# Order of exponential and scaling in a softmax that runs beside a projection

## Chip, cores and metric

The kernel runs on one core of a Trainium2 chip. The metric is the time of one execution on the device in microseconds, the median of several runs. The core has one engine for matrix products (TensorE, PE in the profile, whose weight loads are shown as PEld), three for elementwise work (VectorE or DVE, ScalarE or ACT, GpSimd or POOL) and SyncE (SP), which issues most loads here. Each engine works through its own instructions in the order in which the program gives them; semaphores tie the engines together.

## The reference

One layer of a transformer on 256 tokens of width 1024: eight heads of blockwise attention of width 64 and four heads of retention of width 128 side by side, gated and merged, then a feed-forward block with a short convolution, each followed by a layer norm. With 256 tokens and a block of 256 there is one block, so the attention is plain causal attention:

```
l_own = jnp.einsum('bhqd,bhkd->bhqk', qc, k_own).astype(jnp.float32) * scale
l_own = jnp.where(causal, l_own, NEG_BIG)
...
p = jax.nn.softmax(logits, axis=-1).astype(v.dtype)
p_own = p[..., :MOBA_BLOCK]
...
return (jnp.einsum('bhqk,bhkd->bhqd', p_own, v_own) + ...)
```

What the change touches is the softmax of these eight heads.

## The kernel before

The program is one list of about 60 and more **steps** of matrix products over streamed weights (`steps`), and beside it generators (`sides`) that add small work between them. A weight tile of 128 x 2048 (`raw`, four buffers) is loaded by SyncE, split into two halves, and each half into a high part `whi` (ScalarE, line 1264) and a rest `wlo` (VectorE, line 1278), so that products have more than the precision of one pass. A buffer of `raw` is loaded again as soon as VectorE has read its last half; some loads (`in_ada`) feed a product on VectorE alone (line 263). The loop at line 1320 prepares halves some five ahead of their use, and `whi` one more ahead.

Steps 0 to 15 are the projections to queries and keys (`wstat_rot`, TensorE lines 134 and 138). Each pair of steps uses two of the four banks 0 to 3 of the accumulator memory in turn, and ScalarE copies each result out (line 504). Two steps of this kind hold 16 matmuls of line 134 and 16 of line 138. From step 16 on come steps of 12 matmuls (lines 123 to 125): `winB`, `winGa`, `winGr`. Rotations of the projected heads run on VectorE (lines 1006 to 1012).

The attention is the generator `mixers` (line 1029). Each step calls it three times, and its loop variable `i` is the step less 7 (`SCORES_AT`). The first call does nothing. The second, ahead of the step's matmuls in program order, holds ScalarE's exponentials and scalings. The third, behind the matmuls, holds VectorE's reciprocals, TensorE's transposes and scores, and VectorE's maxima:

- `scores(h)` (line 1050) forms the scores of four heads in banks 4, 7, 5, 6.
- `maxima(h)` (line 1059) adds the mask and scale for two heads, writes the scores out of the banks into a buffer of six heads (`sms`), and takes the row maxima.
- The exponential (line 1086) of a head subtracts the maximum and sums the rows; the reciprocal (line 1090) inverts the sums; the scaling (line 1082) multiplies the head by it.
- The transposes (line 1098) turn a head's scaled probabilities through a bank, and line 1100 copies them out. `attend` (line 1072) multiplies them by the values, at `i = 12`, after step 19. `retention` (from line 1114) follows and uses banks 4, 7, 0, 1 and then 5, 6.

In the kernel before, at each `i` the head `i - 2` is scaled and then head `i - 1` gets its exponential. Heads 0 and 1 are transposed at `i = 5` (step 12), 2 to 5 at 8 (step 15), 6 and 7 at 10 (step 17). Maxima are taken at `i = 0, 2, 4, 5`.

Of the kernel before, what the change touches and what calls it, by code (L numbers as in the profile page):

```python
# [9 lines left out]
AF = mybir.ActivationFunctionType  # L10
# [3 lines left out]
HM, DM = 8, 64  # L14
# [54 lines left out]
def _body(nc, a, out, pe, act, dve, sp, cst, wts, big, tmp, ps, dram):  # L69
    f = lambda ap: ap.bitcast(F32)  # L70

    def bank(i):
        return ps.tile([128, 512], F32, tag=f"P{i}", name=f"P{i}")
# [10 lines left out]
    def slot(n, shape, dt=F32):  # L84
        if n in pairs:
            assert pairs[n].dtype == dt
            return pairs[n].rearrange("p e (k t) -> p e k t", k=shape[2])
        if n not in place:
            return big.tile(shape, dt, tag=f"A{n}", name=f"A{n}")
        pair, e = place[n]  # L90
        assert pairs[pair].dtype == dt
        v = pairs[pair][:, e, :math.prod(shape[1:])]
        return v.rearrange("p (a b) -> p a b", a=shape[1]) if len(shape) == 3 else v
# [5 lines left out]
    def split(hi, lo, src):  # L99
        act.activation(hi, src, AF.Copy)  # L100
        dve.tensor_tensor(lo, src, f(hi), OP.subtract)
# [927 lines left out]
    def mixers():  # L1029


        for _ in range(3 * SCORES_AT):
            yield
        v = S["v"]
        S["decay"] = [slot(n, [128, 2, 384]) for n in ("6a", "6b")]
        for i in range(2):
            nc.gpsimd.dma_start(S["decay"][i], a["decay"][i])
        st, pt = {}, {}
        blk = [slice(128 * qb, 128 + 256 * qb) for qb in range(2)]

        def scores(h):


            S["sc"] = [bank(b) for b in (4, 7, 5, 6)]
            x = S["rot"][h // 4]
            for qb, c in enumerate(blk):
                for i in range(2):
                    for e in range(4):
                        s = slice(32 * e, 32 * e + 32)
                        pe.matmul(S["sc"][e][:, c], x[s, i, qb * 128:(qb + 1) * 128], x[s, 2 + i, :128 + 128 * qb],  # L1050
                                  start=i == 0, stop=i == 1)

        def maxima(h):

            for e in range(2):
                sm = S["sms"][:, (h + e) % (TL + 2)]
                mx = tmp.tile([128, 8], F32, name="mx", bufs=TL + 2)
                for qb, c in enumerate(blk):
                    dve.tensor_tensor_reduce(out=sm[:, c], in0=S["sc"][h % 4 + e][:, c],  # L1059
                                             in1=consts["mask"][:, 128 - 128 * qb:],  # L1060
                                             scale=-0.125, scalar=3.0e38, op0=OP.add, op1=OP.min,
                                             accum_out=mx[:, 2 + qb:3 + qb])
                st[h + e] = sm, mx

        def attend(h, p):

            for w in range(2):
                pT = [pt.pop(h + 2 * w + e) for e in range(2)]
                for kb, (o, c) in enumerate(((slice(0, 256), slice(0, 256)), (slice(128, 256), slice(256, 384)))):
                    for e in range(2):  # L1070
                        u = h + 2 * w + e
                        pe.matmul(p[64 * e:64 * e + 64, 256 * w + o.start:256 * w + o.stop],  # L1072
                                  v[:, kb, 64 * u:64 * u + 64], pT[e][:, c], start=kb == 0, stop=kb == 1)
            return lambda: split(S["yah"][:, h // 2:h // 2 + 2], S["yal"][:, h // 2:h // 2 + 2],
                                 p.rearrange("p (w t) -> p w t", w=2))

        for i in range(HM + 5):
            yield
            if 0 <= i - 2 < HM:
                sm, mx = st[i - 2]  # L1080
                for qb, c in enumerate(blk):
                    act.activation(sm[:, c], sm[:, c], AF.Copy, scale=mx[:, 6 + qb:7 + qb])
            if 0 <= i - 1 < HM:
                sm, mx = st[i - 1]
                for qb, c in enumerate(blk):
                    act.activation(sm[:, c], sm[:, c], AF.Exp, scale=-1.0, bias=mx[:, 2 + qb:3 + qb],
                                   accum_out=mx[:, 4 + qb:5 + qb])
            yield
            if 0 <= i - 1 < HM:
                dve.reciprocal(mx[:, 6:8], mx[:, 4:6])  # L1090
            if i == HM + 4:
                S["yah"], S["yal"] = [slot(n, [128, 4, 256], F32R) for n in ("5", "15")]
                done = [attend(4 * g, bank(5 + g)) for g in range(2)]
            for h in {5: (0, 1), 8: (2, 3, 4, 5), 10: (6, 7)}.get(i, ()):
                sm, mx = st.pop(h)
                p = bank((4, 7, 4, 7, 5, 6, 5, 6)[h])
                for b in range(3):
                    pe.transpose(p[:, b * 128:(b + 1) * 128], sm[:, b * 128:(b + 1) * 128], ident)
                pT = sm if h > 1 else slot(("9a", "9b")[h], [128, 384])
                act.activation(pT, p[:, :384], AF.Copy)  # L1100
                pt[h] = pT
            if i == 0:
                S["sms"] = slot(11, [128, TL + 2, 384])
            if i in (0, 4):
                scores(i)
            if i in (0, 2, 4, 5):
                maxima(i + i % 2)
            if i == RET_AT:
                sides.append(retention())
            yield  # L1110
        for fn in done:
            fn()
# [192 lines left out]
    prep_to(FIRST + 2)  # L1305
    evac_B()
    sides = [mixers()]

    def run_sides():
# [148 lines left out]
```

## Time and profile before

| | |
|---|---|
| median of 3 runs | 427.67 us (426.02 to 428.06) |
| the profiled execution | 427.91 us |
| its span | 426.2 us |
| mean granted clock of TensorE | 0.996 |
| busy: VectorE, ScalarE, GpSimd | 87%, 59%, 3% of the span |
| bytes read from memory | 104.28 MB, 247 GB/s over the span |

The span runs from the first to the last instruction that the profiler records; what is left of the execution's time lies around it. An engine's busy share is an average over stages; the softmax lies at about 85 to 133 us, and what it costs is read from the waits there. In the rows of the prediction, times are microseconds from the start of the span, `x` counts merged instructions, and `<-` in brackets names what ended an idle time. A row of a merged group gives its first start and the time to its last end; matmuls overlap, so the time that one takes is read from differences of starts.

### The profile page before, as it was taken

To read this page: it belongs to the slowest core of one execution; us is meant where nothing else is said; L and a number is where in the kernel's file an instruction comes from. 1 tells how busy PE (TensorE), PEld (TensorE's weight loads), DVE (VectorE), ACT (ScalarE), POOL (GpSimd) and SP (SyncE) were. 2 spreads that over 40 slices of the span, in tenths; PEclk is the share of its full clock that TensorE was granted. 3 is DMA by queue.
4 is the path that set the end of the run, shared out by engine and by line. 5 is a ranking of instruction groups with operands and counts; after the bars stand their busy time and mean duration, and the time that the engine had idled before them with its cause. 6 is when DMAs were issued, how large, how long until landed. Compare 5 with 4: busy or idle time off the path is not lost.

```text
span 426.2 us, 5934 instructions
## 1 busy us (share of the span) xinstructions
PE 414.9 (97%) x2156; PEld 348.4 (82%) x2156; DVE 370.6 (87%) x593; ACT 252.1 (59%) x442; POOL 14.0 (3%) x26
## 2 busy tenths in 40 slices
PE   7999999997989999999999999999999999999995
PEld 4888888886867888888888888888888888888884
DVE  5979788888988779799788889999999998689996
ACT  4666558658977498635433895374545555456700
POOL 0000010000000100000000000100000000003200
PEclk9999999999989999999999999999999999999999
DMA  8998999675486687979873064796757778550002
GB/s 290 408 408 334 408 397 413 247 245 195 155 297 228 257 304 285 334 269 345 297 256 140 0 235 161 274 363 252 291 211 287 295 250 289 205 197 2 0 2 99
DMA packets 18685, 105.73 MB, mean 248 GB/s; under 512 B 2272, under 2 KB 3680, under 8 KB 7904
## 3 DMA queue, kind: packets, MB, share of 16 engines
q1 hardware_dynamic: 17136, 99.84, 62.5%
q0 software_dynamic: 1376, 4.99, 3.4%
q10 hardware_dynamic: 144, 0.52, 0.5%
q8 instruction: 17, 0.28, 0.2%
q14 instruction: 12, 0.10, 0.1%
HBM read 104.28 MB, written 1.06 MB: 247 GB/s over the span
## 4 chain that ended last, share of the span: by engine, by line
PE 88%; DVE 8%; ACT 2%; DMA 1%; issue 0%; DVEq 0%; ACTq 0%
PE P L134 21%; PE P L337 13%; PE P L123 12%; PE P L125 12%; PE P L124 12%; PE P L138 11%; DVE wlo L1278 2%; DVE junk L263 2%; DMA raw<-in_m 1%; DVE A L1059 1%; PE P L721 1%; PE P L723 1%; PE P L724 1%; PE P L1157 1%; PE P L1072 1%; DVE A8a L1008 1%
## 5 line engine op out<-in xcount | busy, mean ns | idle before, releaser
L1278 DVE TENSOR_TENSOR wlo<-raw,whi 128x1024 fp32r<-128x1024 f32 x118 | 141.8, 1219 | 13.7 <-ACT whi L1264 13.6
L1264 ACT ACTIVATE whi<-raw 128x1024 fp32r<-128x1024 f32 x118 | 121.2, 1055 | 30.9 <-PE P L125 10.5
L134 PE MATMUL P<-AYa,whi 128*128 128x512 f32 x160 | 46.3, 391 | 0.0
L134 PE MATMUL P<-AYb,whi 128*128 128x512 f32 x160 | 43.0, 390 | 0.0
L337 PE MATMUL P<-whi,AH 128*128 128x512 f32 x160 | 41.7, 390 | 0.7 <-DVE AH L303 0.7
L263 DVE CUSTOM_DVE_ANT_0 junk<-raw,srow 128x1024 bf16<-128x1024 f32 x32 | 39.0, 1218 | 0.0
L123 PE MATMUL P<-whi,AH 128*128 128x512 f32 x96 | 38.8, 404 | 0.0
L125 PE MATMUL P<-whi,AH 128*128 128x512 f32 x96 | 37.9, 395 | 0.0
L124 PE MATMUL P<-wlo,AH 128*128 128x512 f32 x96 | 37.9, 394 | 0.0
L337 PEld LDWEIGHTS P<-whi,AH 128*128 128x128 f32 x160 | 29.8, 188 | 8.0 <-ACT whi L320 1.5
L134 PEld LDWEIGHTS P<-AYb,whi 128*128 128x128 f32 x160 | 30.0, 188 | 6.6
L134 PEld LDWEIGHTS P<-AYa,whi 128*128 128x128 f32 x160 | 28.8, 189 | 4.7
L481 ACT ACTIVATE A<-P 128x256 f32<-128x256 f32 x40 | 15.0, 376 | 29.0 <-PE P L138 17.1
L320 ACT ACTIVATE whi<-raw 128x512 fp32r<-128x512 f32 (+1 forms) x26 | 20.8, 824 | 17.8 <-DMA raw<-in_b 16.4
L134 PE MATMUL P<-AH,whi 128*128 128x512 f32 x128 | 31.3, 393 | 0.0
L323 DVE TENSOR_TENSOR wlo<-raw,whi 128x512 fp32r<-128x512 f32 (+1 forms) x26 | 23.6, 935 | 6.2 <-ACT whi L320 5.8
L134 PEld LDWEIGHTS P<-AH,whi 128*128 128x128 f32 x128 | 23.4, 188 | 5.1 <-issue 0.3
L138 PE MATMUL P<-AYb,wlo 128*128 128x256 f32 x160 | 25.7, 283 | 0.0
L138 PE MATMUL P<-AYa,wlo 128*128 128x256 f32 x160 | 25.6, 283 | 0.0
L138 PEld LDWEIGHTS P<-AYa,wlo 128*128 128x128 f32 x160 | 23.3, 190 | 1.6
L337 PE MATMUL P<-wlo,AH 128*128 128x512 f32 x80 | 23.3, 390 | 0.0
L810 DVE SCALAR_TENSOR_TENSOR A<-A,tables 128x255 f32<-128x255 f32 (+1 forms) x44 | 21.3, 483 | 1.6
(310 smaller groups left out, 763.3 us busy)
## 6 DMA issues: line engine op xcount, KB each, us to landing
raw<-in_ada SPq DMA_DIRECT2D x16, 1024.0 KB, 4.8
raw<-in_wup SPq DMA_DIRECT2D x11, 1024.0 KB, 5.2
raw<-in_wgate SPq DMA_DIRECT2D x11, 1024.0 KB, 6.0
raw<-in_wdown SPq DMA_DIRECT2D x11, 1024.0 KB, 5.1
raw<-in_wrot SPq DMA_DIRECT2D x8, 1024.0 KB, 8.1
raw<-in_m SPq DMA_DIRECT2D x4, 1024.0 KB, 8.3
raw<-in_b SPq DMA_DIRECT2D x4, 1024.0 KB, 7.3
raw<-in_winGr SPq DMA_DIRECT2D x4, 1024.0 KB, 4.9
```

The lines of the kernel that those rows point to most:

```text
L123: pe.matmul(o, lh, rh, start=start, stop=False)
L124: pe.matmul(o, lh, rl, start=False, stop=False)
L125: pe.matmul(o, ll, rh, start=False, stop=stop)
L134: pe.matmul(banks()[half], t[0][:, k * 128:(k + 1) * 128], x2(k), start=k == 0, stop=half > 0 and k == 7)
L138: pe.matmul(banks()[half][:, :256], t[1][:, k * 128:(k + 1) * 128], x2(k)[:, 0], start=False, stop=half == 0 and k == 7)
L263: dve.tensor_tensor_reduce(out=nobody(j if own else None), in0=raw, in1=srow, scale=1.0, scalar=0.0, op0=OP.mult, op1=OP.add, accum_out=mo ...
L320: act.activation(hi[:, o], raw[:, o], AF.Copy)
L323: dve.tensor_tensor(lo[:, o], raw[:, o], f(hi[:, o]), OP.subtract)
L337: pe.matmul(pa[b0 + c // 512 * 2 + t], x[xi][:, j, t * 128:(t + 1) * 128], ws[k][:, c:c + 512], start=first and (xi, k) == (0, 0), stop=la ...
L810: dve.scalar_tensor_tensor(g[:, 2 - n:], x[:, :254 + n], w(n), g[:, 2 - n:], op0=OP.mult, op1=OP.add)
L1264: act.activation(hi, src, AF.Copy)
L1278: dve.tensor_tensor(lo, src, f(hi), OP.subtract)
```

## The change

At each `i` the exponential of head `i - 1` now comes first, and the scaling is that of head `i - 3`. Heads 0 and 1 are transposed at `i = 6` (step 13), 2 to 5 at 9 (step 16), 6 and 7 at 11 (step 18), the last two through banks 4 and 7 instead of 5 and 6. The last maxima come at `i = 6` (step 13) instead of 5. Nothing is added or left out; in the changed kernel line 1082 is the exponential and line 1087 the scaling.

```diff
-            if 0 <= i - 2 < HM:
-                sm, mx = st[i - 2]
-                for qb, c in enumerate(blk):
-                    act.activation(sm[:, c], sm[:, c], AF.Copy, scale=mx[:, 6 + qb:7 + qb])
             if 0 <= i - 1 < HM:
                 sm, mx = st[i - 1]
                 for qb, c in enumerate(blk):
                     act.activation(sm[:, c], sm[:, c], AF.Exp, scale=-1.0, bias=mx[:, 2 + qb:3 + qb],
                                    accum_out=mx[:, 4 + qb:5 + qb])
+            if 0 <= i - 3 < HM:
+                sm, rx = st[i - 3]
+                for qb, c in enumerate(blk):
+                    act.activation(sm[:, c], sm[:, c], AF.Copy, scale=rx[:, 6 + qb:7 + qb])
             yield
             if 0 <= i - 1 < HM:
                 dve.reciprocal(mx[:, 6:8], mx[:, 4:6])
...
-            for h in {5: (0, 1), 8: (2, 3, 4, 5), 10: (6, 7)}.get(i, ()):
+            for h in {6: (0, 1), 9: (2, 3, 4, 5), 11: (6, 7)}.get(i, ()):
                 sm, mx = st.pop(h)
-                p = bank((4, 7, 4, 7, 5, 6, 5, 6)[h])
+                p = bank((4, 7, 4, 7, 5, 6, 4, 7)[h])
...
-            if i in (0, 2, 4, 5):
-                maxima(i + i % 2)
+            if i in (0, 2, 4, 6):
+                maxima(i)
```

Three places show how the instructions move.

On ScalarE at step 11 (`i = 4`), the kernel before has the scaling of head 2 (its sums are in `mx_934`), the exponential of head 3 (`mx_937`), and the two copies of the step's projection:

```order
L1082 ACTIVATE A11_838<-A11_838,mx_934 128x128
L1082 ACTIVATE A11_838<-A11_838,mx_934 128x256
L1086 ACTIVATE A11_838,mx_937<-A11_838,mx_937 128x128
L1086 ACTIVATE A11_838,mx_937<-A11_838,mx_937 128x256
L504 ACTIVATE AR0_584<-P3_961 128x256
```

At the same place of the changed kernel stands the exponential of head 3 (now `mx_935`), then the scaling of head 1 (`mx_862`):

```order
L1082 ACTIVATE A11_838,mx_935<-A11_838,mx_935 128x128
L1082 ACTIVATE A11_838,mx_935<-A11_838,mx_935 128x256
L1087 ACTIVATE A11_838<-A11_838,mx_862 128x128
L1087 ACTIVATE A11_838<-A11_838,mx_862 128x256
L504 ACTIVATE AR0_584<-P3_959 128x256
```

The exponential has gone ahead of a scaling, and that scaling is of an older head.

On TensorE at steps 12 and 13, the kernel before has the transposes of heads 0 and 1 (line 1098, three to a head) between the two steps of a projection:

```order
L134 MATMUL P_1048<-AH,whi 128x512 x8
L134 MATMUL P_1049<-AH,whi 128x512
L138 MATMUL P_1048<-AH,wlo 128x256 x8
L1098 MATMUL P_1070<-ident,A_838 128x128 x3
L1098 MATMUL P_1076<-ident,A_838 128x128 x3
L138 MATMUL P_1049<-AH,wlo 128x256 x8
L134 MATMUL P_1049<-AH,whi 128x512 x7
```

The changed kernel has them behind both steps:

```order
L134 MATMUL P_1046<-AH,whi 128x512 x8
L134 MATMUL P_1047<-AH,whi 128x512
L138 MATMUL P_1046<-AH,wlo 128x256 x8
L138 MATMUL P_1047<-AH,wlo 128x256 x8
L134 MATMUL P_1047<-AH,whi 128x512 x7
L1098 MATMUL P_1093<-ident,A_838 128x128 x3
L1098 MATMUL P_1099<-ident,A_838 128x128 x3
```

Fifteen matmuls have moved ahead of the six transposes.

On ScalarE at steps 15 to 19, the kernel before copies out the transposes of heads 2 to 5 (line 1100), splits two halves of the second `winGa` load (`raw_1117`) with the scaling of head 7 between them, copies out heads 6 and 7, and then splits the first `winGr` load (`raw_1201`):

```order
L1100 ACTIVATE A11_838<-P4_1177 128x384
L1100 ACTIVATE A11_838<-P7_1182 128x384
L1100 ACTIVATE A11_838<-P5_1187 128x384
L1100 ACTIVATE A11_838<-P6_1192 128x384
L1264 ACTIVATE whi_1197<-raw_1117 128x1024
L1082 ACTIVATE A11_838<-A11_838,mx_1085 128x128
L1082 ACTIVATE A11_838<-A11_838,mx_1085 128x256
L1264 ACTIVATE whi_1225<-raw_1117 128x1024
L1100 ACTIVATE A11_838<-P5_1249 128x384
L1100 ACTIVATE A11_838<-P6_1254 128x384
L1264 ACTIVATE whi_1261<-raw_1201 128x1024
```

The changed kernel has (`raw_1115` is the second `winGa` load, `raw_1179` the first `winGr` load, `mx_1105` and `mx_1108` are heads 6 and 7):

```order
L1264 ACTIVATE whi_1175<-raw_1115 128x1024
L1087 ACTIVATE A11_838<-A11_838,mx_1105 128x128
L1087 ACTIVATE A11_838<-A11_838,mx_1105 128x256
L1100 ACTIVATE A11_838<-P4_1203 128x384
L1100 ACTIVATE A11_838<-P7_1208 128x384
L1100 ACTIVATE A11_838<-P5_1213 128x384
L1100 ACTIVATE A11_838<-P6_1218 128x384
L1264 ACTIVATE whi_1223<-raw_1115 128x1024
L1087 ACTIVATE A11_838<-A11_838,mx_1108 128x128
L1087 ACTIVATE A11_838<-A11_838,mx_1108 128x256
L1264 ACTIVATE whi_1251<-raw_1179 128x1024
L1100 ACTIVATE A11_838<-P4_1271 128x384
```

The first half of the second `winGa` load now stands ahead of the copies of heads 2 to 5 and of the scaling of head 6, and the first half of `winGr` ahead of the copies of heads 6 and 7. On VectorE the maxima of heads 6 and 7 stand behind the rotation's lines 1010 and 1012 and one reciprocal, where they stood ahead of them; nothing else changes there. SyncE and GpSimd have the same order as before.

## The prediction

> **What bounds the kernel now.** I read the page's shares of busy time first, then who waited for whom on TensorE over the whole span.
>
> ```profile
> PE 414.9 (97%) x2156; PEld 348.4 (82%) x2156; DVE 370.6 (87%) x593; ACT 252.1 (59%) x442; POOL 14.0 (3%) x26
> PE P L1098 <- DVE mx L1059: 2.3, 1, 2.3
> PE P L228 <- DVE srow L226: 1.6, 1, 1.6
> PE P L1098 <- ACT A L1082: 1.1, 1, 1.1
> PE P L1098 <- ACT A L1100: 0.9, 1, 0.9
> PE P L337 <- DVE AH L303: 0.7, 1, 0.7
> PE P L885 <- ACT AYb L883: 0.4, 1, 0.4
> ```
>
> TensorE is busy 97% of the span, and three of its six waits, 4.3 us together, stand ahead of L1098: the transposes of the probabilities. Of the other three, two lie in the opening and one near the end. Between the softmax and the end TensorE waits for nothing more, so what it gains here should reach the end whole. Next comes the timeline of TensorE around the waits (start, length, instruction, idle before it in brackets).
>
> ```profile
> 102.99 1.11 PE L138 MATMUL P<-AH,wlo 128*128 128x256 f32 x8
> 106.40 1.16 PE L1098 MATMUL P<-ident,A 128*128 128x128 f32 x6 [2.30 <-DVE mx L1059]
> 108.36 3.82 PE L134 MATMUL P<-AH,whi 128*128 128x512 f32 x16
> 112.02 2.08 PE L138 MATMUL P<-AH,wlo 128*128 128x256 f32 x16
> 113.93 1.78 PE L134 MATMUL P<-AH,whi 128*128 128x512 f32 x7
> 115.55 1.49 PE L1098 MATMUL P<-ident,A 128*128 128x128 f32 x12
> 116.80 0.48 PE L123 MATMUL P<-whi,AH 128*128 128x512 f32 x1
> 122.14 0.39 PE L125 MATMUL P<-whi,AH 128*128 128x512 f32 x1
> 123.41 0.55 PE L1098 MATMUL P<-ident,A 128*128 128x128 f32 x3 [0.88 <-ACT A L1100]
> 125.02 1.08 PE L1098 MATMUL P<-ident,A 128*128 128x128 f32 x3 [1.07 <-ACT A L1082]
> 125.75 0.78 PE L123 MATMUL P<-whi,AH 128*128 128x512 f32 x1
> 128.88 0.39 PE L124 MATMUL P<-wlo,AH 128*128 128x512 f32 x1
> 132.85 0.43 PE L1072 MATMUL P<-A9a,A 128*64 128x256 f32 x1
> ```
>
> The first wait stands before the transposes of heads 0 and 1, the others before heads 6 and 7. The 24 matmuls from 116.80 step by 0.23 us; after the third wait the seven between 125.75 and 128.88 take 3.13 us, 0.45 each. The windows say why (busy time of each engine, granted clock, DMA).
>
> ```profile
> 106.00:108.00 2.00, 1.50 (x11) 1.29 (x12) 2.00 (x9) 2.00 (x4) 0.00 (x0) 1.00 0.99 418
> 126.00:128.00 2.00, 2.00 (x6) 1.55 (x6) 2.00 (x4) 1.22 (x4) 0.00 (x0) 0.50 0.60 254
> ```
>
> Behind the late waits the granted clock fell to 0.50, behind the first it stayed at 1.00: a further loss of 3.13 - 7 x 0.23, about 1.5 us. I take L1072 at 132.85, the first matmul on the transposed probabilities, as the mark by which the change is measured.
>
> Behind the first wait is a ping-pong of VectorE and ScalarE, shown by VectorE's timeline:
>
> ```profile
> 103.74 0.16 DVE L1090 RECIPROCAL mx<-mx 128x2 f32<-128x2 f32 x1
> 105.64 0.17 DVE L1090 RECIPROCAL mx<-mx 128x2 f32<-128x2 f32 x1 [1.74 <-ACT A L1086]
> 111.55 0.16 DVE L1090 RECIPROCAL mx<-mx 128x2 f32<-128x2 f32 x1
> 112.72 1.22 DVE L1010 TENSOR_TENSOR AR<-AR,A8b 128x1024 f32<-128x1024 f32 x1
> 115.27 1.20 DVE L1278 TENSOR_TENSOR wlo<-raw,whi 128x1024 fp32r<-128x1024 f32 x1
> 121.72 0.17 DVE L1090 RECIPROCAL mx<-mx 128x2 f32<-128x2 f32 x1 [1.75 <-ACT A L1086]
> ```
>
> The reciprocal of head 2 (103.74) releases head 2's scaling on ScalarE; head 3's exponential stands behind that scaling, and VectorE waits 1.74 us for it before head 3's reciprocal and the maxima that the transposes need. At 121.72 it happens again with heads 6 and 7.
>
> **Part one, the exponential ahead of the scaling.** ScalarE at the same place, with the scaling of head 2 and the two projection copies of that step:
>
> ```profile
> 103.93 0.80 ACT L1082 ACTIVATE A<-A,mx 128x128 f32<-128x128 f32 x2 [2.10 <-DVE mx L1090]
> 105.52 0.36 ACT L504 ACTIVATE AR<-P 128x256 f32<-128x256 f32 x1
> 105.78 0.36 ACT L504 ACTIVATE A<-P 128x256 f32<-128x256 f32 x1
> ```
>
> The same 16 exponentials and 16 scalings run, so ScalarE's own work stays: 105.52 - 103.93 = 1.59 us for one scaling and one exponential, of which 0.69 is the scaling (rows below) and 0.9 the exponential. What changes is the wait. ScalarE was free at 103.93 - 2.10 = 101.83. In the changed order as much work stands ahead of head 3's exponential as stood ahead of head 2's scaling, and its maxima are a step old; it starts by 101.83 and ends by 102.7, a us before VectorE comes to its reciprocals at 103.74. The 1.74 goes. Four maxima take 112.72 - 111.55 - 0.08 = 1.09, so those of heads 4 and 5 stand at 104.0 to 105.1. All later VectorE work moves up by 1.74, and behind the second ping-pong, which breaks in the same way, by 1.74 + 1.75 = 3.49.
>
> **Part two, transposes a step later.** Those of heads 0 and 1 now follow eight L138 (half of 113.93 - 112.02, 0.96) and seven L134 (115.55 - 113.93, 1.62) more. TensorE, done with the row at 102.99 by 103.95, reaches them at 103.95 + 0.96 + 1.62 = 106.5; the maxima that empty their banks have ended at 105.1. The 2.30 goes, covered by 1.4 us. If the ping-pong stayed, the maxima would end at 106.8 and 0.3 would come back.
>
> **Part three, maxima of heads 6 and 7 behind a rotation.** On VectorE the L1010 and L1012 work (112.72 to 115.19, 2.47 us) now goes first. The reciprocal at 111.55 becomes 109.8; the rotation ends at 112.4, head 6's half of the maxima at 112.9. ScalarE comes there about as late: from 101.83 stand three pairs of exponential and scaling (1.59 each), three pairs of copies (0.53), four weight halves (0.94) and two evacuations (0.37), 10.9 us, so 112.7; it waits a little for the maxima. Behind that wait are two exponentials with two scalings and two copies, 1.59 + 0.53 + 1.59, so head 5's scaling ends at 116.6. TensorE comes to head 5's transposes at 106.5 + 0.63 + 5.59 + 2.78 + 0.94 = 116.4: half of the 12 transposes' 1.25 (115.55 to 116.80), a unit of nine and seven L134 and sixteen L138 (3.66 x 9/16 + 1.91 + 1.62), 12 matmuls (half of 122.37 - 116.80) and three quarters of the 1.25. With a handover of 0.2, I charge 0.4 us there. The bounds are 0, if ScalarE is early, and 0.9, if maxima and copies both come half a us later. Four banks rotate under the projections, so late copies hold up nothing else.
>
> **Part four, the end of the softmax.** Here ScalarE's order matters: the front matter shows weight halves (L1264) ahead of the scalings of heads 6 and 7 and of the last evacuations.
>
> ```profile
> 122.12 1.62 ACT L1100 ACTIVATE A<-P 128x384 f32<-128x384 f32 x4
> 123.60 1.08 ACT L1264 ACTIVATE whi<-raw 128x1024 fp32r<-128x1024 f32 x1
> 124.54 0.82 ACT L1082 ACTIVATE A<-A,mx 128x128 f32<-128x128 f32 x2
> 125.23 1.07 ACT L1264 ACTIVATE whi<-raw 128x1024 fp32r<-128x1024 f32 x1
> 127.84 2.01 ACT L1264 ACTIVATE whi<-raw 128x1024 fp32r<-128x1024 f32 x2 [0.78 <-DMA raw<-in_winGr]
> 116.53 0.33 SPq L110 DMA_DIRECT2D raw<-in_winGa  x1
> 123.07 0.33 SPq L110 DMA_DIRECT2D raw<-in_winGr  x1
> DMA to landing us min/median/max: 4.9/5.5/6.2
> raw<-in_wrot SPq DMA_DIRECT2D x8, 1024.0 KB, 8.1
> ```
>
> The half at 123.60 is the first of the second winGa load. That load is issued at 116.53, when L1278 at 115.27 has freed a raw buffer. With VectorE 1.74 earlier it is issued at 114.8 and lands, by the two winGa loads' 4.9 to 6.2 us (the row of landings is theirs), at 119.7 to 121.0; I take 120.3, the median. ScalarE has done the copies behind head 5's scaling by 117.2 and stands idle, so the half starts on landing. From there, by differences of starts above: half 0.94, scaling 0.69, four evacuations 1.48, half 0.94, scaling of head 7 0.69: 4.74 us, and 0.4 for its last two transposes. So the next matmul starts 5.15 after landing: 125.45 (124.85 to 126.15). TensorE would reach head 7 at 116.4 + 0.31 + 0.4 + 5.57 + 0.3 = 123.0 (head 5's transposes with their wait, 24 matmuls, head 6's transposes) and idles about 2.1 us. **The three waits become one, which ends on a transfer.** Only one step of 12 matmuls remains, 2.78, then L1072 at 128.3 (127.7 to 129.0) with 0.07 of handover, against 132.85: a gain of 4.55 (3.85 to 5.15).
>
> The last evacuations now stand behind the first winGr half. Its issue at 123.07 moves by 3.49 to 119.6; before, it landed at 127.84, 4.8 from issue, so now at 124.4, and ScalarE reaches it at 125.1 or later: hidden. Evacuations end by 127.5, ahead of the mark. Banks 4 and 7, now used by heads 6 and 7, are emptied by the same evacuations. SyncE's and GpSimd's orders are unchanged.
>
> **The clock.** An idle of 2.1 us is as long as the 1.95 of the two late waits, after which 1.5 us were lost; the 2.30 of the first wait left the clock at 1.00. Bounds 0 and 1.5; being between a case that fell and one that did not, I take the middle, 0.75. [...]
>
> **Sum.** The profiled execution took 427.91 us, a span of 426.2 and 1.7 around it, 0.24 over the median of 427.67. 427.91 - 4.55 + 0.75 = 424.1. Own range: 427.91 - 5.15 = 422.8 without clock loss and early landing, 427.91 - 3.85 + 1.5 = 425.6 with both late.
>
> **Rivals.**
> A, the forecast: 0.68.
> B, no wait at the end. If the winGa load lands by 118, L1072 comes at 123.0 + 0.35 + 2.85 = 126.2, a gain of 6.65: 421.3. Against it: a landing 3.2 us after issue, where 4.9 is the shortest of its kind. 0.10.
> D, VectorE is not freed: ScalarE comes late to head 3's exponential, so the first 1.74 stays, and the change mostly fails to do what it says. Then the load is issued at 116.53, lands at 121.4 to 122.7, L1072 comes 8.0 later at 129.4 to 130.7; with a certain clock loss the gain is 1.95 to 0.65: 426.0 to 427.3. For it: two weight halves stand ahead on ScalarE at that place; against: ScalarE waits 2.10 us there now, and the changed order adds nothing ahead. 0.16.
> C, slower: the winGa transfer, put where ScalarE idles, is late. With the 1.5 of clock, L1072 passes 132.85 once it lands after 123.35, 8.6 us from issue; each us more is one lost. The wrot loads took a median of 8.1 when several ran at once; at 12 us the time is 427.91 + 3.4 = 431.3. Against it: the kernel's two winGa loads landed within 6.2. 0.06.
>
> **How the numbers follow.** A measurement of this kernel can tell about 0.5%, 2.1 us, from no change, so faster means below 425.5. A's greatest part and B lie there: 0.77. D, A's late end and C's first part are within: 0.19. Slower 0.04. The range, 422.0 to 426.6, leaves out B, D's late end and C, together about 0.2.
>
> **What would show it.** Right: no idle before the transposes of heads 0 and 1; no VectorE wait for an exponential at either reciprocal pair; the winGa issue near 114.8; ScalarE idle before a half with a DMA as releaser; one TensorE idle of about 2 us before head 7's transposes; L1072 near 128 to 129. Wrong: a wait of head 3's reciprocal, a wait of projection matmuls for a bank, a winGa landing outside 119.7 to 121.0, or new TensorE idle after L1072.

## The result and the profile after

The changed kernel takes 423.82 us (median of 8 runs, 422.77 to 425.56); the kernel before, beside it on the same chip, took 426.70 (8 runs, 425.83 to 428.06). The ratio is 0.9932 with an interval of 0.9907 to 0.9957: about 0.7% faster. The profiled execution took 425.56 us, with a span of 423.8. TensorE's busy time and its waits over the whole span, from the page of the changed kernel and its list of waits (time in all, times, longest):

```profile
PE 414.9 (98%) x2156; PEld 348.3 (82%) x2156; DVE 370.4 (87%) x593; ACT 252.1 (59%) x442; POOL 14.0 (3%) x26
PE P L1098 <- ACT A L1087: 1.8, 1, 1.8
...
PE P L1098 <- ACT A L1100: 0.7, 1, 0.7
...
```

Of the three waits ahead of L1098 the 2.3 us for the maxima is gone; the two others, for a copy and a scaling of ScalarE, have grown from 2.0 to 2.5 us together. TensorE's timeline around them:

```profile
106.46 0.82 PE L1098 MATMUL P<-ident,A 128*128 128x128 f32 x6
115.44 1.47 PE L1098 MATMUL P<-ident,A 128*128 128x128 f32 x12
123.09 0.55 PE L1098 MATMUL P<-ident,A 128*128 128x128 f32 x3 [0.69 <-ACT A L1100]
125.47 1.08 PE L1098 MATMUL P<-ident,A 128*128 128x128 f32 x3 [1.83 <-ACT A L1087]
126.21 0.78 PE L123 MATMUL P<-whi,AH 128*128 128x512 f32 x1
129.29 0.40 PE L124 MATMUL P<-wlo,AH 128*128 128x512 f32 x1
130.53 0.43 PE L1072 MATMUL P<-A9a,A 128*64 128x256 f32 x1
138.95 0.59 PE L1143 MATMUL P<-A2a,A 128*128 128x256 f32 x2
```

The transposes of heads 0 and 1 (106.46) and of heads 2 to 5 (115.44) now start without an idle. The mark L1072 has come from 132.85 to 130.53, by 2.32. A second mark is more telling in what follows: L1143, retention's values, some 8 us behind L1072. In the kernel before it stood here:

```profile
141.28 0.59 PE L1143 MATMUL P<-A2a,A 128*128 128x256 f32 x2
```

It moved by 2.33, and the execution by 427.91 - 425.56 = 2.35: what is won there reaches the end whole. VectorE's reciprocals, with no idle ahead of either pair:

```profile
103.67 0.22 DVE L1090 RECIPROCAL mx<-mx 128x2 f32<-128x2 f32 x2
117.97 0.22 DVE L1090 RECIPROCAL mx<-mx 128x2 f32<-128x2 f32 x2
```

The ping-pong's 1.74 and 1.75 are gone. What took its place is on ScalarE:

```profile
120.92 1.06 ACT L1264 ACTIVATE whi<-raw 128x1024 fp32r<-128x1024 f32 x1 [3.97 <-DMA raw<-in_winGa]
...
122.57 1.61 ACT L1100 ACTIVATE A<-P 128x384 f32<-128x384 f32 x4
124.05 1.07 ACT L1264 ACTIVATE whi<-raw 128x1024 fp32r<-128x1024 f32 x1
125.00 0.81 ACT L1087 ACTIVATE A<-A,mx 128x128 f32<-128x128 f32 x2
126.33 1.06 ACT L1264 ACTIVATE whi<-raw 128x1024 fp32r<-128x1024 f32 x1 [0.51 <-DMA raw<-in_winGr]
```

SyncE's issues of the two loads, and the granted clock (third value from the end of a window's row):

```profile
114.70 0.33 SPq L110 DMA_DIRECT2D raw<-in_winGa  x1
118.08 0.33 SPq L110 DMA_DIRECT2D raw<-in_ada  x1
119.38 0.33 SPq L110 DMA_DIRECT2D raw<-in_winGr  x1
126.00:128.00 2.00, 2.00 (x6) 1.68 (x7) 1.97 (x4) 1.67 (x3) 0.00 (x0) 0.50 0.94 250
```

ScalarE stands 3.97 us before a weight half whose load was issued at 114.70 and landed at 120.92. Scalings and copies that could have run meanwhile are queued behind it, and TensorE waits for them. After its idle the clock is 0.50 again.

### The profile page after: what moved, and what is told of

It is laid out like the page before. It is cut to its first block, busy times and chain, and to the rows that moved or that the text cites. A ratio compares the mean times of both kernels' runs of the same rounds, so it can differ in the third digit from the quotient of the medians.

```text
span 423.8 us, 5941 instructions
## 1 busy us (share of the span) xinstructions
PE 414.9 (98%) x2156; PEld 348.3 (82%) x2156; DVE 370.4 (87%) x593; ACT 252.1 (59%) x442; POOL 14.0 (3%) x26
## 4 chain that ended last, share of the span: by engine, by line
PE 87%; DVE 7%; DMA 2%; ACT 2%; issue 0%; DVEq 0%; ACTq 0%
PE P L134 21%; PE P L337 13%; PE P L123 12%; PE P L124 12%; PE P L125 12%; PE P L138 11%; DVE wlo L1278 2%; DMA raw<-in_winGa 1%; DVE junk L263 1%; DMA raw<-in_m 1%; PE P L721 1%; PE P L723 1%; PE P L724 1%; DVE A L1059 1%; PE P L1157 1%; PE P L1072 1%
```

## The experiments

The theory was the prediction's: the exponential ahead of the scaling breaks the ping-pong and carries the gain; what is left is ScalarE standing at a weight half. The rival was that the later places of the transposes carry it. The diffs are against the kernel named; durations are read as before, and experiments on the changed kernel have their lines shifted by 4.

### The swap alone

Against the kernel before: the scaling keeps head `i - 2`, and transposes and maxima keep their places.

```diff
-            if 0 <= i - 2 < HM:  # scaling of head i - 2
...
             if 0 <= i - 1 < HM:  # exponential of head i - 1
...
+            if 0 <= i - 2 < HM:
+                sm, rx = st[i - 2]
+                for qb, c in enumerate(blk):
+                    act.activation(sm[:, c], sm[:, c], AF.Copy, scale=rx[:, 6 + qb:7 + qb])
```

> Only the swap: the exponential of head i-1 goes ahead of the scaling of head i-2; transposes and maxima stay where they were before. Theory (the gain comes from breaking the ping-pong of VectorE and ScalarE, and ends at the wait for the winGa landing): both VectorE waits for an exponential (1.74 and 1.75 us) are gone; the wait before the transposes of heads 0 and 1 falls from 2.30 to about 1.1 us, since the maxima of heads 4 and 5 still end at 105.1; the winGa load is issued at 114.7; a wait of about 1.6 us stays before the transposes of head 7; L1072 at 128.6 us at full clock, 130.1 with the clock's loss, so 0 to 0.5 us from the changed kernel, about 423 to 425 us. Rival (the later transposes carry the gain): at least 1.5 us slower than the changed kernel, and close to the kernel before.

Measured: 423.56 us (6 runs, 423.25 to 424.07), ratio 0.9922 (0.9903 to 0.9940). TensorE's timeline:

```profile
104.10 1.17 PE L1098 MATMUL P<-ident,A 128*128 128x128 f32 x6 [0.45 <-DVE mx L1059]
...
114.79 0.83 PE L1098 MATMUL P<-ident,A 128*128 128x128 f32 x3 [0.41 <-ACT A L1087]
...
122.01 0.83 PE L1098 MATMUL P<-ident,A 128*128 128x128 f32 x3 [0.56 <-ACT A L1087]
...
136.66 0.59 PE L1143 MATMUL P<-A2a,A 128*128 128x256 f32 x2
```

The swap alone gives what the full change gives; the intervals overlap almost wholly. The first wait falls from 2.30 to 0.45 (1.1 expected) with the transposes where they were, since VectorE no longer waits 1.74 us ahead of the maxima that empty their banks. A wait of 0.41 stands ahead of head 5's transposes (114.79); the kernel before and the changed kernel have none there. The last wait is 0.56, less than the 1.6 I expected and less than the 2.5 of the full change: with the early places, the copies of heads 2 to 5 stand on ScalarE ahead of the weight half, not behind it.

### The later places alone

Against the kernel before: the table of transposes, the banks and the places of the maxima as in the change, the scaling still first.

```diff
-            for h in {5: (0, 1), 8: (2, 3, 4, 5), 10: (6, 7)}.get(i, ()):
+            for h in {6: (0, 1), 9: (2, 3, 4, 5), 11: (6, 7)}.get(i, ()):
...
-            if i in (0, 2, 4, 5):
-                maxima(i + i % 2)
+            if i in (0, 2, 4, 6):
+                maxima(i)
```

> Only the later places: transposes and last maxima as in the changed kernel, but the scaling of head i-2 still ahead of the exponential of head i-1. Theory: both VectorE waits stay at about 1.7 us; the wait before the transposes of heads 0 and 1 falls to 0.3 to 0.5 us; the winGa load is issued at 116.5; the last wait, now 2 to 2.5 us, comes from the copies of heads 2 and 3 behind the weight half; L1072 at 128.4 to 129 us at full clock, 1.5 later with the loss; 423 to 425.5 us, so either part alone gives most of the gain and the two do not add. Rival (the swap carries the gain): within 0.5 us of the kernel before, by runs of the same clock.

Measured: 425.23 us (7 runs, 425.14 to 425.87), ratio 0.9963 (0.9947 to 0.9979). The kernel before took 426.49 beside both this kernel and the swap: the later places alone gain 1.26 us where the swap gains 2.93, somewhat under half. That is the slow end of the 423 to 425.5 that my theory gave; that either part alone gives most of the gain is not borne out, and the rival's 0.5 us or less from the kernel before is not either. VectorE and TensorE:

```profile
105.36 0.17 DVE L1090 RECIPROCAL mx<-mx 128x2 f32<-128x2 f32 x1 [1.75 <-ACT A L1086]
121.50 0.17 DVE L1090 RECIPROCAL mx<-mx 128x2 f32<-128x2 f32 x1 [1.75 <-ACT A L1086]
124.07 0.93 PE L1098 MATMUL P<-ident,A 128*128 128x128 f32 x6 [1.09 <-ACT A L1100]
127.70 0.43 PE L1072 MATMUL P<-A9a,A 128*64 128x256 f32 x1
137.68 1.28 DVE L101 TENSOR_TENSOR A<-P,A 128x512 fp32r<-128x512 f32 x2
138.51 0.67 PE L1143 MATMUL P<-A2a,A 128*128 128x256 f32 x2 [1.10 <-DVE A L101]
```

Both waits of the ping-pong stay. The first wait of TensorE is gone, the last is 1.09 (2 to 2.5 expected), and L1072 comes at 127.70, as early as in the best profile of the full change below. But VectorE, not freed, comes to its L101 at 137.68, 3.36 later than in the third of the changed kernel's further profiles below; L1143 waits 1.10 us for it, and stands at 138.51 against the swap's 136.66. So what VectorE gains is needed behind the softmax, and L1072, 127.70 here, is too early a mark to judge by.

### The scalings of heads 6 and 7 ahead of the weight halves

Against the changed kernel: at the top of the loop, before the first `yield`, and out of their old place.

```diff
+            if i in (9, 10):
+                sm, rx = st[i - 3]
+                for qb, c in enumerate(blk):
+                    act.activation(sm[:, c], sm[:, c], AF.Copy, scale=rx[:, 6 + qb:7 + qb])
             yield
...
-            if 0 <= i - 3 < HM:
+            if 0 <= i - 3 < HM - 2:
```

> The changed kernel with the scalings of heads 6 and 7 put ahead of the weight half of their step on ScalarE. Theory (the last wait is ScalarE standing at a weight half whose load has not landed): the load is issued at 114.7 and lands at about 120.9 as in the changed kernel; head 7's scaling ends at about 124.0 instead of 125.7, the idle ahead of the transposes of heads 6 and 7 falls from 2.5 to about 1.3 us, L1072 at 127.4 us at full clock; 1.0 to 1.4 us faster than the changed kernel by runs of the same clock, and fewer runs with a clock under 0.998. Rival (ScalarE's amount of work sets the wait): no gain, since the same instructions stand ahead of head 7's transposes in sum.

Measured: 422.89 us (5 runs, 422.19 to 423.20), ratio to the kernel before 0.9902 (0.9883 to 0.9921). TensorE's timeline:

```profile
122.95 0.83 PE L1102 MATMUL P<-ident,A 128*128 128x128 f32 x3 [0.46 <-ACT A L1081]
126.48 0.43 PE L1072 MATMUL P<-A9a,A 128*64 128x256 f32 x1
136.23 0.59 PE L1147 MATMUL P<-A2a,A 128*128 128x256 f32 x2
```

The idle ahead of the last transposes (L1102 here; L1081 is the scaling in its new place) fell from 2.5 to 0.46, further than the 1.3 expected; in the third further profile of the changed kernel below, whose load landed about as early as here, it was 1.61. What TensorE waited for there was the place of the scalings in ScalarE's order.

The time follows only in part. L1072 came at 126.48, 1.23 earlier than in that profile, but L1147, which is L1143 of the changed kernel, did not: 136.23 against 136.14. Behind the mark TensorE now waits 0.48 us at L1161 for L517, a gate's activation on ScalarE. The median fell by 0.9, and the intervals of the two ratios overlap. The changed kernel's eight runs lie in two groups, four from 422.77 to 423.32 and four from 424.32 to 425.56; the five runs here are hardly faster than its lower group, where 1.0 to 1.4 us were expected, and what they gain is that none lies in the upper one.

### The weight half one step later as well

Against the last: the high half is not prepared ahead during step 16.

```diff
-            ahead = first() if live[0] + 2 <= HL_BUFS else None
+            ahead = first() if live[0] + 2 <= HL_BUFS and S["main"] != 16 else None
```

> As the run with the early scalings, and the weight half of the second winGa load is taken one step later on ScalarE, so that nothing of heads 2 to 7 stands behind it until the copies of heads 6 and 7. Theory: no TensorE idle ahead of any transpose; L1072 at 125.9 us; perhaps 0.2 us ahead of the products of heads 6 and 7, whose copies stand behind the first winGr half; mean clock at least 0.999 in every run, so the two groups of times 1.7 us apart become one; 420.0 to 421.3 us, 2.5 to 3 us faster than the changed kernel's runs at full clock. Rival for the last wait (ScalarE's amount of work): the idle stays above 1.5 us. Rival for the two groups of times (something other than the idle lowers the clock): runs at 0.994 to 0.996 remain about half.

Measured: 422.91 us (5 runs, 422.51 to 422.94), ratio 0.9901 (0.9883 to 0.9919). No gain on the last, where 1.5 us or more were expected. ScalarE and TensorE:

```profile
126.73 1.06 ACT L1268 ACTIVATE whi<-raw 128x1024 fp32r<-128x1024 f32 x1 [3.81 <-DMA raw<-in_winGr]
122.13 0.82 PE L1102 MATMUL P<-ident,A 128*128 128x128 f32 x6
128.22 1.25 PE L1072 MATMUL P<-A,A 128*64 128x256 f32 x8 [0.41 <-ACT A L1104]
131.45 2.06 PE L1161 MATMUL P<-AR 64*128 64x256 f32 x16 [0.48 <-ACT A7a L517]
136.30 0.59 PE L1147 MATMUL P<-A2a,A 128*128 128x256 f32 x2
```

The wait ahead of the transposes is gone, as the theory says, but ScalarE now stands 3.81 us at the next weight half, the first of `winGr`, with the copies of heads 6 and 7 and retention's L517 queued behind it. TensorE pays 0.41 and 0.48 there, and L1147 stands where it stood (136.30 against 136.23). The mean granted clock is 0.998 to 1.000 in all five runs, where the changed kernel's upper four have 0.994 to 0.996: with the idle, the upper group is gone. One run is below the 0.999 that I expected of each.

### The winGr half later too

Against the last: that half, too, behind the copies and L517.

```diff
-            ahead = first() if live[0] + 2 <= HL_BUFS and S["main"] != 16 else None
+            ahead = first() if live[0] + 2 <= HL_BUFS and S["main"] not in (16, 18) else None
...
-            prep_to(max(need) + 1 + (... NEAR if s < NEAR_TO else ...
+            prep_to(max(need) + 1 + (... NEAR - (s == 19) if s < NEAR_TO else ...
```

> As the run without the block, and the first winGr halves are also taken later on ScalarE, behind the copies of heads 6 and 7, the gate's activations (L517, L519) and the first pass over the attended values. Theory (the run without the block gave its gain back to the first winGr half, whose load landed at 126.7 and held the copies of heads 6 and 7, 0.41 us of wait, and the release of banks 0 and 1 by L517, 0.48, then VectorE's part of the retention): all three waits go, the first product of the retention's values comes at 134.2 us instead of 136.30, and the time is 420.5 to 421.4 us. Rival (something else, such as VectorE's own queue, now sets the retention): the product stays at 136 or later, 422.5 us or more.

Measured: 421.37 us (5 runs, 421.17 to 422.49), ratio 0.9871 (0.9848 to 0.9894): the best version, faster than both kernels. TensorE:

```profile
134.27 0.59 PE L1147 MATMUL P<-A2a,A 128*128 128x256 f32 x2
199.56 0.63 PE L555 MATMUL P<-ident,A 128*128 128x128 f32 x4 [0.35 <-DVE A L564]
```

No wait for the softmax is left, and L1147 came 2.03 earlier. The time fell by 1.54 only. From L1147 to the end of the span of 420.0 are 285.7 us, where the changed kernel's third further profile has 421.0 - 136.14 = 284.9. At 199.56 stands a wait of 0.35 for VectorE that that profile doesn't show, where part of the gain is given back. The product came at 134.27 (134.2 expected) and the median lies within the 420.5 to 421.4 expected; two runs, 421.68 and 422.49, lie above.

### The idle filled

Against the changed kernel: nine matmuls into a bank that nobody reads (line 1097), ahead of the transposes of heads 6 and 7. They are extra work; if it is the idle that drops the clock, they cost nothing beside it and keep the clock.

```diff
+            if i == 11:
+                unused = bank(2)
+                for _ in range(9):
+                    pe.matmul(unused, hh[:, 0, :128], h1x2[:, :, 0], start=True, stop=True)
             for h in {6: (0, 1), 9: (2, 3, 4, 5), 11: (6, 7)}.get(i, ()):
```

> The changed kernel with nine more matmuls of 0.23 us into a bank that nobody reads, ahead of the transposes of heads 6 and 7, where TensorE idled 2.5 us. Theory (the changed kernel's two groups of times, 422.8 to 423.3 and 424.3 to 425.6 us, differ by whether the idle lowers the clock): the added 2.05 us lie in the idle, the transposes of head 7 come at the same time as before the addition, the clock stays at full there, and all runs fall into one group at 422.8 to 423.6 us, with mean clocks of 0.998 or more. Rival (the groups come from something else): two groups about 1.7 us apart as before. If the added work did not fit the idle: all runs later by up to 2 us.

Measured: 423.08 us (6 runs, 422.89 to 423.99), ratio 0.9911 (0.9893 to 0.9929). TensorE:

```profile
122.08 2.21 PE L1097 MATMUL P<-AH 128*128 128x512 f32 x9
...
127.85 0.43 PE L1072 MATMUL P<-A9a,A 128*64 128x256 f32 x1
```

L1072 comes at 127.85, as early as an execution of the changed kernel without clock loss (below), no window is at half clock (each from 100 to 132 us has 1.00), and no run passes 424.0, where four of the changed kernel's eight do. One run, 423.99, lay outside what was expected, and two had a mean clock of 0.997, just below the 0.998 expected. If each run had the changed kernel's chance of about a half, six in a row without a fall would come once in 64. So the fall belongs to the idle, as far as six runs can show it; the intervals of the two ratios alone overlap.

### Further profiles of both kernels

One profile can't show what varies between executions, so the kernel before was profiled once more and the changed kernel three times, unchanged.

> The kernel before, unchanged, for a second profile. Its runs fall into 426.0 to 426.5 and 427.5 to 428.1 us. If the profile is of the lower group, theory: the waits before the transposes are the same 2.3, 0.9 and 1.1 us, and the stretch at half clock either is absent or lies where TensorE waits, with L1072 near 131.4 instead of 132.85. Rival: a wait is shorter by 1.5 us.

Measured: 425.94 us. TensorE of the kernel before, and a window behind its first wait:

```profile
106.04 1.54 PE L1098 MATMUL P<-ident,A 128*128 128x128 f32 x6 [2.31 <-DVE mx L1059]
123.21 0.49 PE L1098 MATMUL P<-ident,A 128*128 128x128 f32 x3
124.67 0.83 PE L1098 MATMUL P<-ident,A 128*128 128x128 f32 x3 [0.96 <-ACT A L1082]
130.91 0.43 PE L1072 MATMUL P<-A9a,A 128*64 128x256 f32 x1
106.00:108.00 2.00, 1.96 (x9) 1.85 (x10) 2.00 (x6) 2.00 (x4) 0.00 (x0) 0.50 0.84 352
```

Here the clock fell behind the first wait, not the late ones. TensorE came late to head 6's transposes, and the 0.88 of the other profile is gone: the lost clock was taken out of a wait that would have come anyway. This I had not expected; I had all three waits as fixed. L1072 stands 1.94 earlier than in the other profile of the same kernel.

> The changed kernel, unchanged, for a second profile. If it is of the lower group (422.8 to 423.3 us): the wait before the transposes of head 7 is the same 1.8 us within 0.5, no matmul behind it runs at half clock, and L1072 is at 129.0 instead of 130.53. Rival: the winGa load lands earlier and the wait is shorter by 1.5 us.

> The changed kernel, unchanged, for a profile of its lower group of times (422.8 to 423.3 us), which the two profiles so far (425.56 and 425.38) have not shown. Theory: if the time is in the lower group, the wait before the transposes of head 7 is still 1 to 2 us, no window behind it has a granted clock of 0.50, and L1072 is at 128.0 to 129.2 us. Rival: the wait is absent because the winGa load landed early, before 118 us.

> The same as the run before it, in case that one falls into the upper group again (424.3 to 425.6 us): lower group, theory as there; upper group, a window at 0.50 behind the transposes of head 7 and L1072 at 130 us or later.

Measured: 425.38, 424.50 and 422.76 us. In the first two the clock fell behind the late idle (0.50 and 0.51 in the window from 126 to 128), in the third it did not (1.00). The second:

```profile
124.38 0.83 PE L1098 MATMUL P<-ident,A 128*128 128x128 f32 x3 [1.83 <-ACT A L1087]
129.48 0.43 PE L1072 MATMUL P<-A9a,A 128*64 128x256 f32 x1
126.00:128.00 2.00, 2.00 (x6) 1.59 (x5) 1.97 (x4) 1.61 (x3) 0.00 (x0) 0.51 0.78 274
```

The third, with ScalarE's weight half and VectorE's L101:

```profile
124.19 0.83 PE L1098 MATMUL P<-ident,A 128*128 128x128 f32 x3 [1.61 <-ACT A L1087]
127.71 0.43 PE L1072 MATMUL P<-A9a,A 128*64 128x256 f32 x1
136.14 0.59 PE L1143 MATMUL P<-A2a,A 128*128 128x256 f32 x2
126.00:128.00 2.00, 2.00 (x12) 1.35 (x12) 1.97 (x4) 1.77 (x4) 0.00 (x0) 1.00 0.96 287
119.64 1.07 ACT L1264 ACTIVATE whi<-raw 128x1024 fp32r<-128x1024 f32 x1 [2.88 <-DMA raw<-in_winGa]
134.32 1.28 DVE L101 TENSOR_TENSOR A<-P,A 128x512 fp32r<-128x512 f32 x2
```

Idles of 1.83 and 1.61 us, near each other, and in between the same matmuls: L1072 follows the transposes by 5.10 us in one and by 3.52 in the other, 1.58 apart. That is the price of the clock, and it accounts for most of the 1.74 between the two runs. In the second of these profiles TensorE worked again from 124.38, with the clock at 1.00 in the window from 124 to 126; it fell only at about 126, some 1.6 us behind the end of the idle.

## Why the prediction was right

**The outcome.** It was rival A, the forecast: the three waits became one idle around the transposes of heads 6 and 7, and it ends on a transfer. The time, 423.82 against 424.1, and all 8 runs lie in the range. That the time came within 0.3 us is partly luck. I counted from the profiled execution of 427.91 and took off 3.8 us, where the medians side by side differ by 426.70 - 423.82 = 2.9: a start 1.2 too high and a gain 0.9 too large, which nearly cancel. That execution was a long one of the kernel before, with the clock lost behind the late waits and nothing to absorb it. And the 0.75 us that I took for the clock is a middle that hardly any execution shows: no run lies between 423.32 and 424.32, and the median of eight is the middle of these two.

**Part one** was right in mechanism and sizes: both idles ahead of reciprocals are gone, and the winGa load was issued at 114.70 (114.8 forecast). The swap alone shows that this part brings as much as the whole change does.

**Part two** was right as a reading of the changed kernel: transposes of heads 0 and 1 at 106.46 (106.5), without a wait. As a reason for the gain it was not needed: the swap alone leaves 0.45 of the 2.30. By themselves the later places do bring 1.26 us, so the two parts overlap.

**Part three**: the 0.4 at head 5's transposes was 0. The twelve transposes at 115.44 take 1.47, where they took 1.49 before; the lower of its bounds held. ScalarE came to head 6's exponential at 111.39, not at 112.7, and waited 1.24 us for the maxima instead of a little: I had let head 3's exponential start at 101.83, and it started at 100.44. At `i = 2` no head is scaled yet in the changed order, so that one scaling less, 0.69 us, stood ahead of it; that is part of the difference.

**Part four** was right in its main steps. The half started on landing, at 120.92 (119.7 to 121.0), and the next matmul 5.29 after it (5.15). The third further profile, where the load landed at 119.64, has it at 124.78, 5.14 after. The idle was 0.69 + 1.83 = 2.52 (2.1). Its first piece, ahead of head 6's transposes, wasn't in the forecast: they use bank 4 now, and the copy that empties it stands behind the half. Where the load landed earlier, at 119.64, this piece is absent. L1072 in that third profile, at full clock, is at 127.71 (127.7 to 129.0), a gain of 5.14 over the profile of before, and the span fell by 426.2 - 421.0 = 5.2. One detail was wrong: the first winGr half was to land 4.8 after issue, at 124.4, and to be hidden. It was taken at 126.33, 6.95 after issue. I had looked at its own move alone; `in_ada` was now issued only 1.30 ahead of it. In the changed kernel that costs TensorE nothing visible, but it is the wait that ate the gain of the fourth experiment.

**The clock** was the term of the sum with the largest error in any one execution. The seven matmuls from 126.21 to 129.29 take 3.08 us, 1.47 more than 7 x 0.23; I had taken 0.75 as the middle of 0 and 1.5. Both ends occur, and hardly anything between: four profiles of the changed kernel show the loss three times. For the profiled execution the difference of forecast and result, 3.8 - 2.32 = 1.48, is 0.62 of later landing, 0.14 of the chain behind it and 0.72 of clock.

The length of an idle does not decide alone: 2.30 us left the clock at 1.00 in one profile of before, and 2.31 was followed by 0.50 in the other; 1.83 was followed by 0.51 in the second further profile of the changed kernel, and 1.61 by 1.00 in the third. Each fall lasted as long: in the profile of after the windows of 2 us from 124 to 130 have 0.95, 0.50 and 0.69, which makes 3.4 us at half clock, and the four other falls, two in the kernel before and two in the changed one, come to the same 3.4. Half of that, 1.7 us, is what one fall should cost TensorE if it is busy all through it, an estimate from these windows; between the second and the third further profile 1.58 was measured. That an idle of this length is followed by a fall in some executions only is what the runs show; what decides it was not shown.

**The rivals.** B needed a landing by 118, and the earliest seen is 119.64. C needed one behind 123.35, and the latest is 120.92. D, VectorE not freed, didn't occur in the changed kernel; it is what the later places alone show, and at 425.23 it came out a little under the 426.0 to 427.3 I gave it, without the loss of clock that I had put in.

**What stays open**: why the two parts do not add. The intervals of the swap alone and of the full change overlap, so whether the later places help, cost or do neither by the time can't be told. By the traces the swap alone keeps three short waits, 0.45, 0.41 and 0.56, and its six runs lie together (423.25 to 424.07); the full change has one idle of 1.61 to 2.52 instead. Where the clock held, its L1143 came at 136.14, 0.52 ahead of the swap's 136.66; where it fell, at 138.95 in the first profile. So the later places seem to gain half a us in one kind of execution and to lose more in the other, which no run tested by itself. The 0.8 us that the best version gives back behind L1147 were traced to the wait at 199.56 only in part.

## What to carry to other kernels

Where two in-order engines hand values back and forth, look for an instruction that is ready but stands behind one that is not: here, putting the older work behind the newer (one exponential ahead of one scaling) took away VectorE's waits of 1.74 and 1.75 us without another instruction. Then look at what stands next in the same queue: here it was a weight half whose load had not landed (ScalarE stood 3.97 us at it), and after that the next one (3.81 us), and each had to be moved before the gain showed (422.91 us with the first moved, 421.37 with both). Judge by a mark behind the last wait of the stage, since an earlier one can gain and give it back: with the later places alone L1072 came 5.15 us earlier and L1143 only 2.77.

## What the runs showed of the hardware

In the six profiles of the two kernels an idle of TensorE of some 2 us was followed in some executions by 3.4 us at half clock (worked out from the windows), at 1.5 to 1.6 us lost where it was measured, and not in others of the same kernel. Single idles of 1.83 us (second further profile of the changed kernel) and 2.31 (second profile of the kernel before) were followed by it; others of 1.61 (third further profile) and 2.30 (first profile of the kernel before) were not. In that second profile of the kernel before the clock fell ahead of the late waits, and one of them, 0.88 us in the first, was gone. The second and the third further profile of the changed kernel differ by 1.74 us, of which 1.58 is the clock, so a sum should say with which clock its profile ran.

The first winGr load took longer close behind another. In the kernel before, SyncE issued the load ahead of winGr's here:

```profile
119.92 0.33 SPq L110 DMA_DIRECT2D raw<-in_ada  x1
```

That is 3.15 us ahead of winGr's issue at 123.07, and winGr landed 4.8 us after its issue; in the changed kernel the distance is 1.30 us, and it landed after 6.95. Other profiles agree: with 3.14 us between the two issues winGr landed 4.83 us after its own in the later places alone, and with 1.30 after 6.7 to 7.2 in the changed kernel's three further profiles. Why the load takes longer there was not tried by itself.
